# The inverse of each chunk's system multiplied into alpha and the values' side per unit, and a chain of two steps a chunk

## The chip, the core and the metric

The kernel runs on one core of a Trainium2 chip. The metric is device time in microseconds, from one execution of the whole program; the time before is the median of three runs, 2801.25 us (2798.41 to 2806.16). The core has five engines with queues of their own: TensorE (PE, matmuls), VectorE (DVE), ScalarE (ACT), GpSimd (POOL) and SyncE (SP, which here issues DMAs).

## What is computed

The reference is a trunk of two layers over 1024 positions of width 1024. The second layer's token mixer is a recurrence over positions, of 16 heads with a state of 64x64 each; the change touches only how that recurrence is computed.

```python
def wkv7_scan(r, w, k, v, a_, b_):
    # S_t = S_{t-1} diag(w_t) + (S_{t-1} a_t) b_t^T + v_t k_t^T ;  y_t = S_t r_t
    def step(S, inp):
        r_t, w_t, k_t, v_t, a_t, b_t = inp
        sa = jnp.einsum('bhij,bhj->bhi', S, a_t)
        S = S * w_t[:, :, None, :] + sa[..., None] * b_t[:, :, None, :] + v_t[..., None] * k_t[:, :, None, :]
        y = jnp.einsum('bhij,bhj->bhi', S, r_t)
        return S, y
    ...

def rwkv7_mixer(h, mu, w_in, w0, w1, w2, a0, a1, a2, g1, g2, k_k, k_a, r_k, ln_g, ln_b, w_out):
    ...
    y = wkv7_scan(rh, decay.reshape(B, T, H, N), kh, vh, -kk, kk * ah)
    ...
    return (y * g) @ w_out

    for i in range(DEPTH):
        ...
        if i % N_MIXERS == 0:
            mix = sgu_mixer(h, ...)
        else:
            mix = rwkv7_mixer(h, ...)
        x = x + gate1[:, None, :] * mix
        h = modulate(rms_norm(x), shift2, scale2)
        ff = jnp.square(jax.nn.relu(h @ mlp_w1[i])) @ mlp_w2[i]
        x = x + gate2[:, None, :] * ff
    return rms_norm(x) * final_g
```

## The kernel before

Around the recurrence the program is almost entirely matmuls with streamed weights: adaLN, the first layer and its MLP up to about 1215 us, then the recurrence with other work beside it up to about 2320 us, then the second layer's remaining output projection and MLP. All float32 products of the large matmuls are made from split high and low parts (`wh`, `wl`), three matmuls for one product.

The recurrence (`wkv`) is cut into 16 units: four quarters q of 256 positions (`NQ`, `N`) by four groups m of four heads. A unit has two pairs of heads (z), and each pair four chunks of 64 positions (`CS`). Within a chunk the recurrence is solved as a triangular system: `la` holds the masked products of alpha with the keys' side, `t` and `pf` its inverse, `uv` the solved vectors beside the values, `rr` the masked products for the output, `tm` the transposed key side, `st` or `S` the state.

Per unit there are generators: `unit_a` (decays, alpha and rho into `ar`, the products `pg` in banks g and m, masks into `la` and `rr`), `unit_e` (transposes and centred values), `unit_s` (the inverse of 16x16 blocks on DVE, by way of DRAM), `unit_b` (the inverse's larger blocks, in four half-steps of small matmuls and copies, ending with `pf`), `unit_c` (the chunk chain), `unit_d` (normalisation of the output, with a Ln and an Exp on ACT) and `unit_l` (loads). Each yields the place, in units, at which its next piece is due.

`interleave` merges them with a background generator `bg`: first the projections of the later quarters (`big`, `hidden`, `outs`), with weights read back from DRAM, then the output projection of the first half (`outp`) and most of its MLP (`half0`). A background piece of cost c moves the clock on by c / `RATES`[unit]. So a unit lasts 28.0 of the background's cost numbers (about microseconds of matmul) for the first ten, 41.5 afterwards, and a unit has 13 slots (`SLOT`). PE's instructions are pinned to this order (`Pinned`); the other engines' order is decided by the framework's scheduler, each engine works its own queue in order, and PE's queue waits whole when one operand is late.

The chain before has three steps a chunk, one slot each. In the first, PE adds `la` times `uv` (the values' side) and `ar` times the state into a bank of tag c, and ACT copies it to `xs`. In the second, PE multiplies `xs` by `pf` into tag c, and DVE (one pair) and ACT (the other) copy it to `uv`; the products of rho with the state for the output `y` stand beside it. In the third, PE multiplies `tm` with `uv`, adds `rr` times `uv` to `y`, and DVE makes the new state (`scalar_tensor_tensor` into `S`) from it and `sg`, the decayed state from POOL. Tag c has one buffer.

`outp` of quarter 0 starts when the four units of that quarter are through: `begin_x0` loads the residual into `hm` (tensor `xd`), `gated` reads the units' outputs back (`ev<-yd`), and ACT and DVE split them into `s`.

Of the kernel before, what the change touches and what calls it, by code (L numbers as in the profile page):

```python
# [108 lines left out]
class Trunk:  # L109
# [1074 lines left out]
    SLOT = 1 / 13  # L1184
    RATES = [28.0] * 10 + [41.5]

    def wkv(self, bg):
# [9 lines left out]
        self.ars = [u.tile([P, 8, 3, CS], F32, name=f"ar{i}") for i, u in enumerate(self.ups)]  # L1197
        nc.gpsimd.memset(self.ars[0], 0.0)
# [64 lines left out]
    def unit_0(self):  # L1263
# [11 lines left out]
        yield .5  # L1275
        nc.vector.memset(self.ars[1], 0.0)
# [5 lines left out]
    def unit_a(self, d):  # L1282
# [11 lines left out]
        g = self.own(d, "g", [8, CS + 1], 3)  # L1294
        G.memset(g[:, :, 0:1], 1.0)
        d["ar"] = ar = self.ars[d["n"] % 2]
# [3 lines left out]
        la = self.own(d, "la", [2, 8, CS])  # L1300
# [39 lines left out]
        G.tensor_tensor(ar[:, :, 2], c8(rp), g[:, :, 1:], ALU.mult)  # L1340
# [9 lines left out]
        for z in Z2:  # L1350
            t0 = (6 + z) * self.SLOT
            yield t0
            pg = [self.ps(t) for t in "gm"]
            for c in range(4):
                o = (c ^ z) * P
                cc = z * 4 + c
                for h, s in enumerate(HS):
                    PE.matmul(pg[h][:, o:o + P], bk[s, cc * 2:cc * 2 + 2].rearrange("p a t -> p (a t)"),
                              ar[s, cc, h::2 - h], start=True, stop=True)
# [7 lines left out]
        yield .59  # L1367
# [4 lines left out]
    def unit_e(self, d, z):  # L1372
# [5 lines left out]
        t0 = (8 + 2 * z) * self.SLOT  # L1378
# [8 lines left out]
        yield t0 + self.SLOT  # L1387
# [9 lines left out]
        yield t0 + self.SLOT + .02  # L1397
# [6 lines left out]
    def unit_s(self, d):  # L1404
# [4 lines left out]
        yield 0.61  # L1409
# [5 lines left out]
        yield 0.68  # L1415
        for i in range(1, NB):
# [6 lines left out]
            yield 0.68 + .017 * i  # L1423
        V.tensor_copy(tb[:, 1], tb[:, 0].rearrange("p s k -> p k s"))
        yield 0.96
# [3 lines left out]
        yield 1.0  # L1429
        d["t"] = self.ups[0].tile([P, 8, CS], F32, name="t")  # L1430
        for w, t in enumerate((d["t"], self.own(d, "pf", [8, CS]))):
# [12 lines left out]
    def unit_b(self, d):  # L1444
# [3 lines left out]
        at = lambda i: 1 + i * self.SLOT  # L1448
# [50 lines left out]

    def unit_c(self, d):  # L1500
# [4 lines left out]
        step = lambda i: 1 + (7 + i) * self.SLOT  # L1505
        yield step(0)
        ar, rr, tm, uv, la, pf, g = (d[x] for x in ("ar", "rr", "tm", "uv", "la", "pf", "g"))
# [4 lines left out]
        for c in range(4):  # L1512
# [3 lines left out]
            j = c // 2  # L1516
# [10 lines left out]
            sg = [self.ups[1].tile([P, CS], F32, name="sg", bufs=4) for _ in Z]  # L1527
            gc = [g[:, z * 4 + c, CS:CS + 1] for z in Z]
            for z in Z:
                G.tensor_scalar(sg[z], st[z], gc[z], None, ALU.mult)  # L1530
            yield step(3 * c + 1)
            pu = ht(self.ps("c"))
            for h in range(2):
                for z in Z:
                    PE.matmul(pu[ss[z], h], pf[ss[z], h * 4 + z * 2 + j], xs[ss[z], h], start=True, stop=True)
            for z in Z:
                for h, o in enumerate(HS):
                    PE.matmul(py[o, cc(z)], st[z][o], ar[o, z * 4 + c, 2], start=z == 0, stop=False)
# [11 lines left out]
            for z in Z:  # L1550
                V.scalar_tensor_tensor(ns[z], pq[:, z * CS:z * CS + CS], gc[z], sg[z], ALU.mult, ALU.add)
# [242 lines left out]
```

## Time and profile before

| what | value |
|---|---|
| median of three runs | 2801.25 us |
| the profiled execution | 2805.26 us, of which span 2803.5 us |
| PE busy | 2613.3 us (93%) |
| PEld, DVE, ACT, POOL busy | 2152.6, 1638.3, 1146.9, 544.7 us |
| chain that ended last | PE 67%, DVE 12%, DMA 11%, ACT 4% |
| mean granted clock | 0.969 |

The page gives busy time, a 40-slice map and the chain of waits. The recurrence lies in slices 18 to 33, from about 1215 to 2320 us. The views used are the busy time by stretch, the list of who PE waited for, and the engines' instructions in order of time. A float32 matmul appears there as two pieces, each a load and a matmul; where several pieces of the same kind follow, a row has their count. PE's rows are modelled at their ends, so a cost is read from start to start.

### The profile page before, as it was taken

How to read it: one execution, taken by the hardware profiler on the slowest of the kernel's cores; microseconds unless marked ns; L12 is line 12 of the kernel's file. 1: busy time of each engine (PE TensorE's matmuls, PEld its weight loads, DVE VectorE, ACT ScalarE, POOL GpSimd, SP SyncE). 2: the span in 40 equal slices, each digit the busy share in tenths (PEclk: the TensorE clock that was granted, in tenths of full speed). 3: DMA queues.
4: the chain of work that ended last, by engine and by line, in shares of the span. 5: the costliest groups of instructions: out<-in, count | busy, mean ns of one | idle time of the engine just before them, and what ended most of it. 6: DMA issues, size and time to landing. Idle time of an engine off the chain costs nothing.

```text
span 2803.5 us, 49454 instructions
## 1 busy us (share of the span) xinstructions
PE 2613.3 (93%) x19020; PEld 2152.6 (77%) x19020; DVE 1638.3 (58%) x3066; ACT 1146.9 (41%) x2074; POOL 544.7 (19%) x574
## 2 busy tenths in 40 slices
PE   6999999999999999787898997879999999999998
PEld 4788888877888788787787886777777778788887
DVE  7856775444333458866666663566667545744445
ACT  4523442333311344553454543464444334533333
POOL 1000000433300013431322231123334220100001
PEclk9999999999999999998999999899999999999999
DMA  7644545888711354788888889753333324333332
GB/s 279 211 142 128 167 155 163 274 278 255 237 49 49 91 165 138 241 291 261 260 284 265 270 289 274 211 149 110 104 104 100 91 86 151 103 109 94 95 94 83
DMA packets 369708, 483.67 MB, mean 173 GB/s; under 512 B 144320, under 2 KB 153536, under 8 KB 368704
## 3 DMA queue, kind: packets, MB, share of 16 engines
q1 hardware_dynamic: 354496, 454.18, 52.3%
q10 hardware_dynamic: 14976, 26.34, 2.5%
q8 instruction: 149, 2.44, 0.4%
q14 instruction: 87, 0.71, 0.1%
HBM read 390.07 MB, written 90.32 MB: 171 GB/s over the span
## 4 chain that ended last, share of the span: by engine, by line
PE 67%; DVE 12%; DMA 11%; ACT 4%; issue 4%; SPq 1%; POOL 1%; ACTq 0%; DVEq 0%; POOLq 0%
PE acc L448 24%; PE acc L646 15%; PE acc L103 15%; PE c L103 2%; PE acc L503 2%; DMA split<-ada_acc 2%; PE t L103 2%; DMA split<-araw 2%; DVE pr L1420 2%; DVE hm L874 2%; PE acc L894 1%; DVE wl L407 1%; DMA araw<-in_ada_w 1%; DVE xi L440 1%; DMA lb<-ltd 1%
## 5 line engine op out<-in xcount | busy, mean ns | idle before, releaser
L448 PE MATMUL acc<-h,wh 128*128 128x512 f32 x2112 | 667.4, 397 | 0.0
L401 ACT CAST wh<-raw 128x512 fp32r<-128x512 f32 x517 | 318.6, 619 | 732.6 <-PE acc L448 299.0
L646 PE MATMUL acc<-s,wh 128*128 128x512 f32 (+1 forms) x1664 | 510.4, 389 | 12.1 <-DVE s L439 9.1
L407 DVE TENSOR_TENSOR wl<-raw,wh 128x512 fp32r<-128x512 f32 x475 | 363.1, 767 | 264.4 <-ACT wh L401 259.3
L448 PEld LDWEIGHTS acc<-h,wh 128*128 128x128 f32 x2112 | 394.9, 188 | 94.5 <-issue 1.2
L448 PE MATMUL acc<-h,wl 128*128 128x512 f32 x1056 | 418.0, 396 | 0.0
L646 PEld LDWEIGHTS acc<-s,wh 128*128 128x128 f32 x1664 | 308.9, 189 | 86.5 <-DVE s L439 14.8
L646 PE MATMUL acc<-s,wl 128*128 128x512 f32 (+1 forms) x832 | 323.1, 389 | 0.5 <-DVE wl L407 0.5
L452 DVE SCALAR_TENSOR_TENSOR x<-acc,mod,x 128x512 f32<-128x512 f32 (+1 forms) x224 | 163.1, 730 | 231.0 <-PE acc L646 206.4
L448 PEld LDWEIGHTS acc<-h,wl 128*128 128x128 f32 x1056 | 198.4, 188 | 48.0 <-issue 0.5
L103 PE MATMUL acc<-s,wh 128*128 128x512 f32 (+1 forms) x616 | 188.0, 390 | 35.0 <-ACT s L437 18.3
L407 POOL TENSOR_TENSOR wl<-raw,wh 128x512 fp32r<-128x512 f32 (+1 forms) x107 | 145.6, 1363 | 318.2 <-ACT wh L401 156.2
L103 PE MATMUL acc<-xi,wh 128*128 128x256 f32 (+1 forms) x896 | 179.5, 300 | 10.0 <-ACT hm L954 5.2
L646 PEld LDWEIGHTS acc<-s,wl 128*128 128x128 f32 x832 | 157.5, 189 | 35.3 <-DVE wl L407 1.2
L358 POOL TENSOR_TENSOR araw<-araw,ada_acc 128x512 fp32r<-128x512 f32 (+1 forms) x78 | 101.2, 1300 | 389.4 <-ACT ada_acc L355 354.1
L103 PEld LDWEIGHTS acc<-s,wh 128*128 128x128 f32 x616 | 111.0, 196 | 62.8 <-ACT s L437 18.8
L103 PEld LDWEIGHTS acc<-xi,wh 128*128 128x128 f32 (+1 forms) x896 | 144.3, 198 | 17.7 <-ACT hm L954 5.4
L103 PE MATMUL acc<-h,wh 128*128 128x512 f32 (+1 forms) x512 | 150.7, 381 | 3.2 <-ACT ev L1057 3.2
L103 PE MATMUL acc<-xi,wl 128*128 128x256 f32 (+1 forms) x448 | 129.8, 290 | 1.6 <-issue 0.8
L355 ACT CAST ada_acc<-araw 128x512 fp32r<-128x512 f32 (+1 forms) x80 | 49.4, 618 | 168.4 <-DMA split<-ada_acc 124.3
L103 PE MATMUL acc<-s,wl 128*128 128x512 f32 (+1 forms) x308 | 114.9, 373 | 0.0
L157 DVE SCALAR_TENSOR_TENSOR ada_acc<-araw,cond,ada_acc 128x512 f32<-128x512 f32 x140 | 104.4, 746 | 13.0 <-DMA araw<-in_ada_w 11.1
(269 smaller groups left out, 4415.8 us busy)
## 6 DMA issues: line engine op xcount, KB each, us to landing
raw<-in_mlp_w SPq DMA_DIRECT2D x432, 256.0 KB, 2.7
araw<-in_ada_w SPq DMA_DIRECT2D x192, 256.0 KB, 3.5
raw<-split SPq DMA_DIRECT2D x142, 256.0 KB, 4.9
wh<-split SPq DMA_DIRECT2D x141, 256.0 KB, 4.6
wl<-split SPq DMA_DIRECT2D x141, 256.0 KB, 4.7
split<-ada_acc SPq DMA_DIRECT2D x76, 256.0 KB, 3.8
split<-araw SPq DMA_DIRECT2D x76, 256.0 KB, 4.1
araw<-in_w_in SPq DMA_DIRECT2D x48, 256.0 KB, 3.8
```

The lines of the kernel that those rows point to most:

```text
L103: self.tc.keep_in_program_order(self.pe.matmul(*a, **k))
L157: nc.vector.scalar_tensor_tensor(acc, raw, self.cond[:, k:k + 1], acc, ALU.mult, ALU.add)
L355: nc.scalar.copy(hi[:rows, :m].bitcast(F32R), raw[:rows, :m])
L358: nc.gpsimd.tensor_tensor(to[lo, :m].bitcast(F32R), raw[lo, :m], hi[lo, :m], ALU.subtract)
L401: (nc.vector.tensor_copy if self.nhi % 3 == 0 and self.shared else nc.scalar.copy)(wh[:rows], raw[:rows])
L407: eng.tensor_tensor(wl[:rows], raw[:rows], rd(wh[:rows]), ALU.subtract)
L448: nc.tensor.matmul(ps, w[s](k), x[m][:, k], start=n == 0, stop=n == 3 * KC - 1)
L452: self.nc.vector.scalar_tensor_tensor(x[:, e], ps, gate[:, e:e + 1], x[:, e], ALU.mult, ALU.add)
L503: self.nc.tensor.matmul(ps, h[s][:, k, ts], self.wv[k][m], start=k + i == 0, stop=k + i == KC + 1)
L646: nc.tensor.matmul(ps, w[:, k], s[hf, k][:, i, ts], start=n == 0, stop=n == 3 * FB - 1)
L874: nc.vector.scalar_tensor_tensor(t[:, z], self.hx[:, e + z], self.mu[:, i, e + z:e + z + 1], self.h[:, e + z, 1:], ALU.mult, ALU.add)
L1420: V.tensor_tensor(pr[:, :i, :i], lb[:, 0:i, i].unsqueeze(1).to_broadcast([64, i, i]), tb[:, 0, 0:i, 0:i].rearrange("p s k -> p k s"), ALU. ...
```

## The change

Two products that the chain made for each chunk are made for a whole unit, ahead of its chain, by a new generator `unit_x`. It first transposes alpha (bank m, tile `at`) and multiplies `la` by the values' side (bank g, tile `x0`); once `pf` is finished it multiplies `at` by `pf` (banks t and r), which four ACT copies place into `au`, a zeroed tile, and `pf` by `x0` (bank c), which ACT copies to `u0`. The chain's first step is then `au` times the state, with DVE adding `u0` while writing `uv`; `xs` is gone, and a chunk has two steps. The products of rho move into the first step. The other engines' small changes: one full-width multiplication for alpha in place of two half-height ones, and a POOL copy of the chunk-end decays (`gc`). `la`, `pf` and `g` have one buffer, alpha one and rho two.

The grid is ninths of a unit: a chain step is due every 1/9 (it was 1/13), the half-steps of `unit_b` every 1/18 (1/13), the two parts of `pg` 1/9 apart (1/13). The rates go to 27.4 and 42.0. The due places of the other pieces move a little with it: `unit_s` starts 0.04 to 0.06 of a unit later, `unit_d` 0.01 to 0.05 earlier.

```diff
-    SLOT = 1 / 13
-    RATES = [28.0] * 10 + [41.5]
+    SLOT = 1 / 9
+    RATES = [27.4] * 10 + [42.0]
...
-        self.ars = [u.tile([P, 8, 3, CS], F32, name=f"ar{i}") for i, u in enumerate(self.ups)]
-        nc.gpsimd.memset(self.ars[0], 0.0)
+
+        self.ar = ua.tile([P, 3, 8, CS], F32, name="ar")
+
+
+        self.au = ub.tile([P, 4, 2, 2, CS], F32, name="au")
+        nc.gpsimd.memset(self.au, 0.0)
...
-                  self.unit_c(d), self.unit_d(d)]
+                  self.unit_x(d), self.unit_c(d), self.unit_d(d)]
...
-        for i, s in enumerate(HS):
-            V.scalar_tensor_tensor(ar[s, :, i], c8(kk)[s], -(2.0 ** -8), g[s, :, 0:CS], ALU.mult, ALU.mult)
-            yield 0.35 + .02 * i
+        V.scalar_tensor_tensor(al, c8(kk), -(2.0 ** -8), g[:, :, 0:CS], ALU.mult, ALU.mult)
+        yield 0.36
+        G.tensor_copy(gc, g[:, :, CS])
...
-            t0 = (6 + z) * self.SLOT
+            t0 = (4 + z) * self.SLOT
...
-        t0 = (8 + 2 * z) * self.SLOT
+        t0 = (6 + z) * self.SLOT
...
-        at = lambda i: 1 + i * self.SLOT
+        at = lambda i: 1 + (i + 2) / 2 * self.SLOT
...
+    def unit_x(self, d):
+
+
+        nc = self.nc
+        S, PE = nc.scalar, self.pe
+        Z = range(2)
+        HS, LO, HI = self.HS, self.LO, self.HI
+        ss = lambda c, z: HS[c + z & 1]
+        tile = lambda name, *sh: self.ups[0].tile([P, *sh], F32, name=name)
+        yield 8 * self.SLOT
+        la, uv, pf = d["la"], d["uv"], None
+
+        pa = self.ps("m").rearrange("p (c t) -> p c t", c=4)
+        for c in range(4):
+            for z in Z:
+                PE.matmul(pa[ss(c, z), c], self.ar[:, 0, z * 4 + c], self.ident, start=True, stop=True)
+        px = self.ps("g").rearrange("p (c h t) -> p c h t", c=4, h=2)
+        for c in range(4):
+            for h in range(2):
+                for z in Z:
+                    sv = ss(c, 1 - z)
+                    PE.matmul(px[ss(c, z), c, h], la[sv, h, z * 4 + (c ^ z)], uv[sv, z * 4 + c, h], start=True, stop=True)
+        yield 8 * self.SLOT + .015
+        at, x0 = tile("at", 4, P), tile("x0", 4, 2, CS)
+        S.copy(at, pa)
+        S.copy(x0, px)
+        yield 1 + 4.5 * self.SLOT
+        pf = d["pf"]
+
+        pp = [self.ps(t) for t in "tr"]
+        for c in range(4):
+            for i in range(2):
+                for z in Z:
+                    h = (c + z + i) & 1
+                    PE.matmul(pp[i][HS[h], c * CS:c * CS + CS], at[ss(c, z), c, h * CS:h * CS + CS],
+                              pf[ss(c, z), h * 4 + z * 2 + c // 2], start=True, stop=True)
+        pu = self.ps("c").rearrange("p (c h t) -> p c h t", c=4, h=2)
+        for c in range(4):
+            for h in range(2):
+                for z in Z:
+                    PE.matmul(pu[ss(c, z), c, h], pf[ss(c, z), h * 4 + z * 2 + c // 2], x0[ss(c, z), c, h],
+                              start=True, stop=True)
+        yield 1 + 4.5 * self.SLOT + .015
+        for i in range(2):
+            pc = pp[i][:, :4 * CS].rearrange("p (c t) -> p c t", c=4)
+            for h, o in enumerate(HS):
+                S.copy(self.au[o, :, h ^ i, h], pc[o])
+        d["u0"] = tile("u0", 4, 2, CS)
+        S.copy(d["u0"], pu)
...
-        step = lambda i: 1 + (7 + i) * self.SLOT
+        step = lambda i: 1 + (5 + i) * self.SLOT
...
-            px = ht(self.ps("c"))
-            for h in range(2):
-                for z in Z:
-                    sv = ss[1 - z]
-                    PE.matmul(px[ss[z], h], la[sv, h, at(z)], uv[sv, z * 4 + c, h], start=h == 0, stop=False)
-            for h in range(2):
-                for z in Z:
-                    PE.matmul(px[ss[z], h], ar[:, z * 4 + c, h], st[z], start=False, stop=h == 1)
-            xs = self.ups[1].tile([P, 2, CS], F32, name="xs", bufs=2)
-            S.copy(xs, px)
...
-            yield step(3 * c + 1)
             pu = ht(self.ps("c"))
             for h in range(2):
                 for z in Z:
-                    PE.matmul(pu[ss[z], h], pf[ss[z], h * 4 + z * 2 + j], xs[ss[z], h], start=True, stop=True)
+                    PE.matmul(pu[ss[z], h], self.au[:, c, c + z & 1, h], st[z], start=True, stop=True)
...
             for z in Z:
-                (S.copy if z else V.tensor_copy)(uv[ss[z], z * 4 + c], pu[ss[z]])
-            yield step(3 * c + 2)
+                V.tensor_tensor(uv[ss[z], z * 4 + c], pu[ss[z]], u0[ss[z], c], ALU.add)
+            yield step(2 * c + 1)
...
-        yield 2 + 6 * self.SLOT
+        yield 2 + 4 * self.SLOT
```

On PE, around the end of a late unit's inverse and the start of its chain (`r` is the bank of `unit_d`'s matmul with `ysq`, `t` with `w` the last half-step of `unit_b`, rows of `acc` are background). Before:

```order
L103 MATMUL r<-ysq,bones 128x512
L103 MATMUL t<-pf_22787,w_23124 32x32 x16
L103 MATMUL g<-ar_10432,bk 128x128
...
L103 MATMUL c<-uv_22049,la_22050 64x64 x4
L103 MATMUL c<-st_8569,ar_10431 64x64
...
L103 MATMUL c<-xs,pf_22787 64x64 x4
L103 MATMUL y<-ar_10431,st_8569 64x64 x2
```

After:

```order
L103 MATMUL r<-ysq,bones 128x512
L103 MATMUL t<-pf_23240,w_23531 32x32 x16
L103 MATMUL g<-ar,bk 128x128
...
L103 MATMUL t<-pf_23240,at 64x64 x2
L103 MATMUL r<-pf_23240,at 64x64 x2
...
L103 MATMUL c<-x_23147,pf_23240 64x64 x16
...
L103 MATMUL c<-st_8569,au 64x64
L103 MATMUL c<-st_8570,au 64x64
...
L103 MATMUL y<-ar,st_8569 64x64 x2
```

The first product that reads the finished `pf` stands one chain step and two stretches of background behind the last half-step before; now it stands behind `pg` and nine background matmuls, and the chain's first step follows twelve background matmuls later.

On ACT, at the same place of the same unit. `ysq` with TABLE_LOAD ahead is Ln, then Exp, of `unit_d`; `pf` from `t` 32x8x32 is the end of the inverse. Before:

```order
L1488 COPY w_23124<-t 32x256
L401 CAST wh<-raw 128x512
L1572 ACT_TABLE_LOAD
L1572 ACTIVATE ysq<-r,eps_gn 128x512
L1575 ACT_TABLE_LOAD
L1575 ACTIVATE ysq<-ysq 128x512
L1498 COPY pf_22787<-t 32x8x32
L401 CAST wh<-raw 128x512
L1526 COPY xs<-c 128x128
L401 CAST wh<-raw 128x512
L1540 COPY uv_22049<-c 64x128
```

After:

```order
L1493 COPY w_23531<-t 32x256
L401 CAST wh<-raw 128x512
L1615 ACT_TABLE_LOAD
L1615 ACTIVATE ysq<-r,eps_gn 128x512
L1618 ACT_TABLE_LOAD
L1618 ACTIVATE ysq<-ysq 128x512
L1503 COPY pf_23240<-t 32x8x32
L401 CAST wh<-raw 128x512
L1551 COPY au<-t 64x4x64 x2
L1551 COPY au<-r 64x4x64 x2
L1553 COPY u_23651<-c 128x512
```

The copy of `pf` stands behind Ln and Exp in both; now the four copies of `au` and the copy of `u0` stand behind it, ahead of the chain's first step.

On SP, where the output projection of quarter 0 starts: `tpd<-tb` stores the blocks of the inverse that DVE has made, `t<-tpd` and `pf<-tpd` read them back, `hm<-xd` loads the residual, `ev<-yd` the gated outputs, the rest are weights. Before:

```order
L1428 DMA tpd_257<-tb 64x16x16 x2
L326 DMA wl<-split_1_232 128x512
L1133 DMA hm<-xd 128x1024
L1433 DMA t<-tpd_257 64x8x64 x2
L1433 DMA pf_17741<-tpd_257 64x8x64 x2
L1133 DMA hm<-xd 128x1024 x3
L995 DMA ev<-yd_8607 128x512 x3
```

After:

```order
L1133 DMA hm<-xd 128x1024
L1433 DMA tpd_257<-tb 64x16x16 x2
L326 DMA wh<-split_0_225 128x512
L326 DMA wl<-split_1_226 128x512
L1438 DMA t<-tpd_257 64x8x64 x2
L1438 DMA pf_17980<-tpd_257 64x8x64 x2
L326 DMA raw<-split_1_228 128x512
L326 DMA wh<-split_0_229 128x512
L326 DMA wl<-split_1_230 128x512
L326 DMA wh<-split_0_231 128x512
L326 DMA wl<-split_1_232 128x512
L995 DMA ev<-yd_8607 128x512 x3
```

The store and the loads of the inverse, which stood between the last weights and the gated outputs together with all four loads of the residual, now stand five weight loads ahead of them, and one load of the residual there, the others further ahead.

## Rows read from the trace of the kernel before

**Rows 1.** Busy time by stretch: stretch, us, busy us of PE, PEld, DVE, ACT, POOL; PEclk, DMA share, GB/s
```profile
1215.00:1735.00 520.00, 458.83 (x6020) 414.57 (x6020) 316.34 (x784) 252.71 (x500) 134.52 (x162) 0.94 0.88 278
1885.00:2320.00 435.00, 422.31 (x4279) 324.85 (x4279) 266.30 (x591) 182.21 (x352) 152.49 (x163) 0.99 0.37 102
```
**Rows 2.** Who PE waited for, 1215 to 1885 us: us in total, times, longest
```profile
PE acc L103 <- ACT s L437: 20.2, 3, 17.2
...
PE c L103 <- DVE S L1551: 9.5, 8, 2.7
PE c L103 <- ACT uv L1540: 6.4, 4, 3.0
...
PE g L103 <- DVE rr L1365: 3.8, 3, 2.4
```
**Rows 3.** The same view, 1885 to 2320 us
```profile
PE t L103 <- ACT pf L1476: 1.8, 2, 0.9
...
PE c L103 <- ACT uv L1540: 1.5, 1, 1.5
```
**Rows 4.** PE in order of time, one chunk: start us, us, instruction, count
```profile
2271.83 0.63 PE L103 MATMUL acc<-s,wh 128*128 128x512 f32 x2
2272.30 0.39 PE L103 MATMUL acc<-s,wl 128*128 128x512 f32 x1
2272.62 0.45 PE L103 MATMUL c<-uv,la 64*64 64x64 f32 x8
2273.00 0.45 PE L103 MATMUL c<-st,ar 128*64 128x64 f32 x8
2273.38 0.73 PE L103 MATMUL acc<-s,wh 128*128 128x512 f32 x2
2273.95 0.40 PE L103 MATMUL acc<-s,wl 128*128 128x512 f32 x1
...
2276.06 0.40 PE L103 MATMUL acc<-s,wl 128*128 128x512 f32 x1
2276.38 0.45 PE L103 MATMUL c<-xs,pf 64*64 64x64 f32 x8
2276.66 0.40 PE L103 MATMUL y<-ar,st 64*64 64x64 f32 x8
2276.99 0.73 PE L103 MATMUL acc<-s,wh 128*128 128x512 f32 x2
```
**Rows 5.** PE in order of time, six full-width pieces of 128 columns
```profile
1718.22 0.83 PE L103 MATMUL t<-bcent,v 128*128 128x128 f32 x6
1718.81 0.36 PE L103 MATMUL acc<-hr,raw 128*128 128x256 f32 x1
```
**Rows 6.** Busy time by stretch as in rows 1, three stretches after a wait
```profile
1396.90:1403.80 6.90, 6.72 (x104) 6.26 (x106) 2.03 (x4) 0.53 (x2) 4.45 (x6) 0.51 0.96 326
1499.30:1502.80 3.50, 3.50 (x29) 3.38 (x26) 3.47 (x11) 2.10 (x5) 0.00 (x0) 0.51 0.37 140
1564.20:1571.00 6.80, 6.49 (x51) 5.94 (x51) 6.33 (x18) 2.13 (x5) 0.80 (x2) 0.50 0.63 205
```
**Rows 7.** PE, then SP, in order of time, where the first output projection starts
```profile
1751.08 1.31 PE L103 MATMUL acc<-s,wh 128*128 128x256 f32 x2 [17.18 <-ACT s L437]
...
1733.99 1.30 SPq L1428 DMA_DIRECT2D tpd<-tb  x2
...
1743.68 1.52 SPq L995 DMA_DIRECT2D ev<-yd  x3
```
**Rows 8.** ACT in order of time behind one unit's matmul with `ysq`
```profile
1470.49 1.28 ACT L1572 ACT_TABLE_LOAD   x1
1471.79 0.69 ACT L1572 ACTIVATE ysq<-r,eps_gn 128x512 f32<-128x512 f32 x1
...
1474.44 0.36 ACT L1498 COPY pf<-t 32x256 f32<-32x256 f32 x1
```
**Rows 9.** ACT by line and shape: count, busy us, mean ns, idle before it
```profile
L1399 ACT COPY uv<-t 64x256 f32<-64x256 f32 x30 | 11.0, 367 | 34.3 <-PE t L103 33.6 <-ACT ev L985 0.4
```

More of the change, by code (lines that the diff above doesn't have):

```diff
@@ L1293, in unit_a @@
         ew, ea = wa[:, 0], wa[:, 1]
-        g = self.own(d, "g", [8, CS + 1], 3)
+        g = self.own(d, "g", [8, CS + 1], 1)
         G.memset(g[:, :, 0:1], 1.0)
-        d["ar"] = ar = self.ars[d["n"] % 2]
+        pair = slice(0, 2 + d["n"] % 2, 1 + d["n"] % 2)
+        al, rho = self.ar[:, 0], self.ar[:, 1 + d["n"] % 2]
+        d["rho"] = rho
+        gc = self.own(d, "gc", [8])
         rr = self.own(d, "rr", [8, 2, CS])
@@ L1299, in unit_a @@
         self.own(d, "uv", [8, 2, CS])
-        la = self.own(d, "la", [2, 8, CS])
+        la = self.own(d, "la", [2, 8, CS], 1)
         d["bk"] = bk = self.ut.tile([P, 16, CS], F32, name="bk")
@@ L1339, in unit_a @@
         yield .33
-        G.tensor_tensor(ar[:, :, 2], c8(rp), g[:, :, 1:], ALU.mult)
+        G.tensor_tensor(rho, c8(rp), g[:, :, 1:], ALU.mult)
         for z, zs, _, p in Z:
@@ L1358, in unit_a @@
                     PE.matmul(pg[h][:, o:o + P], bk[s, cc * 2:cc * 2 + 2].rearrange("p a t -> p (a t)"),
-                              ar[s, cc, h::2 - h], start=True, stop=True)
+                              self.ar[s, pair, cc], start=True, stop=True)
             yield t0 + .02
@@ L1408, in unit_s @@
         NB = self.NB
-        yield 0.61
+        yield 0.65
         ld = d["ld"]
@@ L1414, in unit_s @@
         pr = self.ups[0].tile([64, NB, NB], F32, name="pr")
-        yield 0.68
+        yield 0.74
         for i in range(1, NB):
@@ L1428, in unit_s @@
             nc.sync.dma_start(self.blocks(td, w), tb[:, w])
-        yield 1.0
+        yield 1.05
         d["t"] = self.ups[0].tile([P, 8, CS], F32, name="t")
-        for w, t in enumerate((d["t"], self.own(d, "pf", [8, CS]))):
+        for w, t in enumerate((d["t"], self.own(d, "pf", [8, CS], 1))):
             for h, s in enumerate(self.HS):
@@ L1504, in unit_c @@
         Z = range(2)
-        step = lambda i: 1 + (7 + i) * self.SLOT
+        step = lambda i: 1 + (5 + i) * self.SLOT
         yield step(0)
-        ar, rr, tm, uv, la, pf, g = (d[x] for x in ("ar", "rr", "tm", "uv", "la", "pf", "g"))
+        rho, rr, tm, uv, u0, gc = (d[x] for x in ("rho", "rr", "tm", "uv", "u0", "gc"))
         at = lambda z: z * 4 + (c ^ z)
@@ L1534, in unit_c @@
                 for z in Z:
-                    PE.matmul(pu[ss[z], h], pf[ss[z], h * 4 + z * 2 + j], xs[ss[z], h], start=True, stop=True)
+                    PE.matmul(pu[ss[z], h], self.au[:, c, c + z & 1, h], st[z], start=True, stop=True)
             for z in Z:
                 for h, o in enumerate(HS):
-                    PE.matmul(py[o, cc(z)], st[z][o], ar[o, z * 4 + c, 2], start=z == 0, stop=False)
+                    PE.matmul(py[o, cc(z)], st[z][o], rho[o, z * 4 + c], start=z == 0, stop=False)
+            sg = [self.ups[1].tile([P, CS], F32, name="sg", bufs=4) for _ in Z]
+            gz = [gc[:, z * 4 + c:z * 4 + c + 1] for z in Z]
             for z in Z:
-                (S.copy if z else V.tensor_copy)(uv[ss[z], z * 4 + c], pu[ss[z]])
-            yield step(3 * c + 2)
+                G.tensor_scalar(sg[z], st[z], gz[z], None, ALU.mult)
+            for z in Z:
+                V.tensor_tensor(uv[ss[z], z * 4 + c], pu[ss[z]], u0[ss[z], c], ALU.add)
+            yield step(2 * c + 1)
             pq = self.ps("c")
@@ L1550, in unit_c @@
             for z in Z:
-                V.scalar_tensor_tensor(ns[z], pq[:, z * CS:z * CS + CS], gc[z], sg[z], ALU.mult, ALU.add)
+                V.scalar_tensor_tensor(ns[z], pq[:, z * CS:z * CS + CS], gz[z], sg[z], ALU.mult, ALU.add)
             st = ns
-            yield step(3 * c + 3) if c < 3 else step(11) + .01
+            yield step(2 * c + 2) if c < 3 else step(7) + .01
         y = d["y"] = self.late("y")
```

31 lines of the change are left out of this document (12 added, 19 removed).

## The prediction

> **What bounds the kernel now.** I read the busy time by stretch first. Over the whole span TensorE (PE) is 93% busy; beside the recurrence it is idle 61 us of 520 up to 1735 us and 13 of 435 from 1885 on [rows 1]. So late units cost what their matmuls cost, and early units that and waits. DMA is at 0.88 in the early stretch, yet few PE waits end on a transfer; the waits list names copies and sums on ACT and DVE. There I look for the waits that the change can move [rows 2, 3]. The chain's own are 9.5 us for the state S (8 waits), 6.4 and 1.5 us for `uv` (5). Next the clock: three stretches right behind such waits, 17.2 us together, ran at 0.50 to 0.51, the level of 1.2 GHz, after PE had stood idle in such a wait, the longest 2.7 and 3.0 us [rows 2, 6]; their matmuls would have needed half the time. Last, one wait has nothing to do with the chain's length: 17.2 us, where the first output projection starts [rows 2, 7].
>
> **The chain's matmuls, taken away: -51 us.** In the late chunk, background matmuls of 512 columns start 0.235 us apart (two take 2271.83 to 2272.30). From the last one before the first step to the next one behind it are 1.08 us, so the step costs 0.85, and 0.10 more because the two matmuls behind it take 0.57 rather than 0.47 [rows 4]. The second step costs 0.93 - 0.235 + 0.10 = 0.80 [rows 4]; the third has as many pieces of the same shape as the second and stays. After the change a first step with `au` (8 pieces, the shape of `st,ar`) and the products of rho (8 pieces, the other shape) replaces two steps. It is built like the old first step, 8 pieces of each shape, so I give it 0.95. That leaves 0.80 a chunk, times 64 chunks.
>
> **The new unit_x on PE: +65 us (58 to 78).** A piece of 64 columns costs 0.029 us when they run two abreast: the 8 of `y` take 0.33 us, less 0.10 to leave [rows 4]. Alone, a piece of 128 columns takes 0.59 / 6 = 0.098 us [rows 5]. First part: the 16 pieces of the transposed alpha, 128 columns in two halves of the output; two abreast 0.8 us, one by one 1.6. Then 32 pieces of `la` with `uv`, 0.93. A change of shape costs 0.10: the 8 pieces of `la` take 0.38 up to `ar`, those of `xs` 0.28 up to `y` [rows 4]. It stands right behind a chain step, so it pays no entrance. Sum 1.85. Second part: 64 pieces at 0.029 make 1.86, entrance and exit 0.33 (what the second step costs beyond its 16 pieces); 2.2, or 1.7 if four pieces of the first half run abreast, in two banks and four quarters of the array, of which no row shows a case. Together 4.05 us a unit (3.6 to 4.9), times 16. I take two abreast, since every group of 64-column pieces in rows 4 does it. PE's net is +14 us (+7 to +27).
>
> A rule speaks against this. The rows show 8 pieces of `xs` by `pf`, from both halves of the partitions into one bank, 0.035 us apart, entrance counted, where one after another they would take 0.05 [rows 4, 5]. The Trainium skill, TensorEngine Tiling (Array Packing), section Restrictions and Gotchas, says that different row tiles cannot access the same PSUM bank simultaneously. By that rule the unit's 96 pieces of 64 columns would cost 4.8 us instead of 2.8, and PE's net would be +46 us instead of +14; the trace speaks against it for the old chain, and the new products are the same shapes.
>
> **The chain's waits: -15 us, and the clock behind them: -8.** A step was due every 28.0 / 13 = 2.15 of the background's cost numbers, and is now due every 27.4 / 9 = 3.04. The same answer of DVE or ACT therefore has two fifths more background to hide behind, and the chunk has two answers instead of three. `uv` now comes from DVE alone, which adds `u0` there. The listed waits of 17.4 us are 1.3 us each on average and 3.0 at most; I keep 2 us (bounds: all stay, none stays). Of the 17.2 us at half clock, half comes back, 8.6; I take 8. The two parts of `pg` move apart in the same way, from 2.15 to 3.04, and the second waits for DVE to empty bank g (3.8 us [rows 2]): -3 (0 to -4).
>
> **The start of the output projection: -10 us (0 to -14).** Before, SP stood until 1733.99 for DVE's blocks (`tpd<-tb`), then issued the inverse's loads and the residual's, and reached `ev<-yd` at 1743.68; PE started at 1751.08 after 17.18 us [rows 7]. With 27.4 for 28.0 the background comes to this place later in the units, and SP has the inverse's store and loads, and three of the residual's four, behind it. Without them the first gated outputs could be asked for about when PE runs dry. What remains is a transfer and a split: 1743.68 to 1751.08 is 7.4 us before, with the residual's loads just ahead. So 7 of 17 stay. What is late next is the third output, whose buffer waits for the last store of a projection.
>
> **New waits: +14 us, and +3 for the clock behind them.** Three places have less cover.
> - The half-steps of the inverse come every 1.52 instead of 2.15. Each needs a copy on ACT or DVE; late units already wait for `pf` there (1.8 us in two waits [rows 3]). I take +5 (0 to +12).
> - The product with finished `pf`. Its copy stands on ACT behind Ln and Exp with their table loads: 4.3 us from the first load to its end [rows 8]. The first load waits for the matmul with `ysq` in ten of 15 units, by the order. PE meanwhile has the 32 pieces of the half-step (0.6 us), `pg` (about 1.2) and 8 to 15 background matmuls, 3.3 to 4.9 us in all. Before, a chain step more stood between, and this copy made no one wait. Now up to 1 us a unit is open: +6 (0 to +15).
> - The four copies into `au`. The nearest row is a 64x256 copy at 0.367 us [rows 9], so 1.5 us, with at times casts between them; PE covers them with the products for `u0` (0.9) and at least 1.4 us of background: +3 (0 to +16).
> The clock can fall behind these as it fell behind the old ones: +3 (0 to +14). DVE and POOL gain and lose small pieces off the path; they cost nothing while DVE is at 61% in both stretches [rows 1].
>
> **Sum.** -51 + 65 - 15 - 8 - 3 - 10 + 14 + 3 = -5 us, against the profiled execution of 2805.26 us, so 2800 there. That execution lay 4.0 us above the median of the three runs, 2801.25; on that scale the forecast is **2796 us**.
>
> **Rivals.**
> - *The cover holds.* The new copies are hidden, the projection starts as soon as its data are there, four pieces run abreast. PE +7, chain waits -17, clock -9, bank g -4, projection -14, new waits +3: -34, so 2767 us. For it: the units whose tables load early need only 3 us. Against it: ACT's queue around the inverse's end is dense.
> - *ACT becomes the bound at the turn of each unit.* If Ln and Exp start late, the copy of `pf` and those of `au` are late in every unit: +15 and +16 in place of +6 and +3, the clock +14 in place of +3. That is 33 us more, 2829 us. It decides from the point where the end of the `pf` copy, 4.3 us behind `ysq`, lies beyond PE's 3.3 to 4.9 us. For it: cover is 3.3 us in several early units. Against it: five of 15 units load the table ahead.
> - *The chain's waits are DVE's queue, not the chain.* Then they stay although a step is dropped, with their clock: 15 + 8 = 23 us more, 2819 us; the change would not do what it says. Against it: the longest wait, 3.0 us, is near what the wider step adds.
> - *The 64-column pieces of unit_x do not pair.* 96 times 0.021 us, 16 units: 32 us more, 2828 us. This is the result of the page's rule above; rows 4 bear against it.
>
> **How the numbers follow.** About 0.3%, 8.4 us, is what a measurement of this kernel can tell from no change. The forecast has 0.55; its own range, 2780 to 2812, holds 0.19 of faster, 0.33 of the same and 0.03 of slower. The cover holds: 0.21, faster. ACT as the bound 0.12, the waits stay 0.08, no pairing 0.04, all slower. So faster 0.40, same 0.33, slower 0.27. The range reaches from the first rival to just beyond the waits that stay, 2768 to 2822; what it leaves out is part of these two ends, about 2 in 10.
>
> **What would show it.** In the profile after: pieces of `c` from `la` and `xs` gone from the chain, one chain step near 0.95 and one near 0.80 us; unit_x near 4 us a unit, its 64-column pieces 0.029 apart; waits for S and `uv` under 3 us in sum; a wait under 10 us at the first `acc<-s` behind 1700 us; waits at the products with `at` and at the chain's first step of about 9 us in sum, released by ACT. The forecast is wrong if those last waits reach 25 us, if idle PE in the early stretch does not fall, or if unit_x costs 6 us.

## The result and the profile after

The changed kernel takes 2824.11 us (median of 6 runs, 2814.04 to 2824.98) where the kernel before, in as many runs beside it, takes 2804.86: ratio 1.0066 (95% interval 1.0049 to 1.0083). On another chip it was 1.0065 (1.0040 to 1.0091). Slower by 19 us; the forecast was 5 us faster.

The profiled execution took 2820.74 us. Its page: span, busy time by engine, the granted clock in tenths.

```profile
span 2819.0 us, 51133 instructions
...
PE 2630.3 (93%) x19788; PEld 2172.3 (77%) x19788; DVE 1650.0 (59%) x3113; ACT 1160.9 (41%) x2057; POOL 544.2 (19%) x590
...
PEclk9999999999999999999989998899999999999999
```

The two stretches of [rows 1], in the same columns:

```profile
1215.00:1735.00 520.00, 460.66 (x6342) 416.76 (x6342) 313.52 (x778) 259.38 (x493) 127.85 (x166) 0.92 0.86 273
1885.00:2320.00 435.00, 416.57 (x4453) 326.00 (x4454) 268.63 (x608) 183.62 (x336) 153.09 (x167) 0.98 0.37 99
```

In this trace PE's idle time beside the recurrence is 59 us early (61 before) and 18 late (13 before), and the clock is lower in both. In the two later traces of the changed kernel the early stretch has 69 us idle (63 in the second of before), at the clock of before, 0.94. Whom PE waited for, 1215 to 1900 us (total us, times, longest), answers [rows 2]:

```profile
PE acc L103 <- ACT s L437: 16.8, 2, 10.8
...
PE c L103 <- ACT u L1553: 10.5, 4, 7.6
...
PE t L103 <- ACT pf L1503: 3.2, 4, 1.2
...
PE c L103 <- DVE uv L1583: 2.3, 5, 0.8
PE t L103 <- ACT w L1467: 2.2, 2, 2.0
PE t L103 <- ACT pf L1481: 2.0, 4, 1.0
...
PE c L103 <- DVE S L1594: 0.7, 2, 0.4
```

The same, 1900 to 2340 us, answers [rows 3]:

```profile
PE t L103 <- ACT pf L1481: 5.3, 2, 3.3
PE t L103 <- ACT w L1467: 3.9, 1, 3.9
PE t L103 <- ACT pf L1503: 2.8, 4, 1.5
```

The chain's waits went as planned: 17.4 us for S and `uv` became 3.0. The wait for bank g's `rr` is gone. In their place, where one unit's inverse ends and its chain begins (the turn of the unit), stand 30 us: 13.4 in the half-steps (`pf` L1481, `w`), 6.0 at the product with finished `pf` (L1503), and 10.5 at the chain's first matmul, for `u`.

That last one was not in the forecast, and 7.6 of its 10.5 us stand at a single turn of the sixteen. PE in order of time there:

```profile
1536.66 0.27 PE L103 MATMUL t<-pf,at 64*64 64x64 f32 x2
1536.67 0.27 PE L103 MATMUL r<-pf,at 64*64 64x64 f32 x2
...
1537.17 1.10 PE L103 MATMUL c<-x,pf 64*64 64x64 f32 x32
1538.20 1.61 PE L103 MATMUL acc<-xi,raw 128*96 128x256 f32 x12
1547.44 0.69 PE L103 MATMUL c<-st,au 128*64 128x64 f32 x8 [7.63 <-ACT u L1553]
```

ACT in the same stretch (in brackets how long it stood idle ahead of the instruction, and for whom):

```profile
1535.47 0.63 ACT L1618 ACTIVATE ysq<-ysq 128x512 f32<-128x512 f32 x1
1536.13 0.37 ACT L1503 COPY pf<-t 32x256 f32<-32x256 f32 x1
1541.07 0.62 ACT L437 CAST xi<-hm 128x512 fp32r<-128x512 f32 x1 [4.57 <-DVE hm L874]
1541.71 0.36 ACT L1551 COPY au<-t 64x256 f32<-64x256 f32 x1
...
1544.70 0.41 ACT L437 CAST hr<-hm 128x256 fp32r<-128x256 f32 x1 [1.05 <-DVE hm L955]
1545.13 0.37 ACT L1551 COPY au<-r 64x256 f32<-64x256 f32 x1
1546.16 0.62 ACT L437 CAST xi<-hm 128x512 fp32r<-128x512 f32 x1 [0.66 <-DVE hm L874]
1546.80 0.58 ACT L1553 COPY u<-c 128x512 f32<-128x512 f32 x1
```

The product is finished at 1538.2, and ACT is idle, yet its copies stand behind casts of the background, which wait for DVE: 4.57, 1.05 and 0.66 us. DVE in the same stretch:

```profile
1536.14 2.08 DVE L1622 SCALAR_TENSOR_TENSOR ysq<-y,bvec,ysq 128x256 f32<-128x256 f32 x2 [1.62 <-ACT ysq L1618]
1538.15 1.26 DVE L1625 SCALAR_TENSOR_TENSOR ysq<-ysq,bvec,v 128x256 f32<-128x256 f32 x1
...
1539.99 1.78 DVE L874 SCALAR_TENSOR_TENSOR hm<-hm,mu 128x256 f32<-128x256 f32 x4
```

It is at the previous unit's group norm, which waited for ACT's own Exp, and comes to `hm` behind it. The chain's first matmul needs bank c, which `pu` holds until the copy `u` has read it.

### The profile page after: what moved, and what is told of

Read it like the earlier page. It is cut to its first block, busy times and chain, and to the rows that moved or that the text cites. A ratio compares the mean times of both kernels' runs of the same rounds, so it can differ in the third digit from the quotient of the medians.

```text
span 2819.0 us, 51133 instructions
## 1 busy us (share of the span) xinstructions
PE 2630.3 (93%) x19788; PEld 2172.3 (77%) x19788; DVE 1650.0 (59%) x3113; ACT 1160.9 (41%) x2057; POOL 544.2 (19%) x590
## 4 chain that ended last, share of the span: by engine, by line
PE 66%; DMA 12%; DVE 11%; ACT 5%; issue 4%; SPq 1%; POOL 1%; ACTq 0%; DVEq 0%; POOLq 0%
PE acc L448 24%; PE acc L646 16%; PE acc L103 15%; DMA split<-araw 2%; DMA split<-ada_acc 2%; PE t L103 2%; PE acc L503 2%; DVE pr L1425 2%; PE c L103 1%; PE g L103 1%; DVE wl L407 1%; DVE hm L874 1%; DMA araw<-in_ada_w 1%; DMA wl<-split 1%; PE acc L894 1%
## 5 line engine op out<-in xcount | busy, mean ns | idle before, releaser
L103 PEld LDWEIGHTS acc<-xi,wh 128*128 128x128 f32 (+1 forms) x896 | 144.8, 199 | 20.2 <-ACT ev L989 7.8
L103 PE MATMUL acc<-xi,raw 128*128 128x256 f32 (+1 forms) x672 | 101.5, 298 | 12.3 <-ACT hm L954 6.0
```

The costliest lines, as they stand in the source:

```text
L103: self.tc.keep_in_program_order(self.pe.matmul(*a, **k))
```

## Where the time went

Both programs have the same 11,020 background matmuls, so the trace can be cut at the same ones. The table takes the time between the starts of the 4350th and the 9600th (1108 and 2481 us before) apart: idle stretches of PE above 0.15 us; half of PE's time at half clock, idle stretches left out; the time from a background matmul's start to the next one's where small ones stand between, less these two; the rest. The third kind holds the background matmul ahead of each interruption, which cancels in the table, with 226 interruptions before and 225 after. Before is the mean of two traces, after of three.

| us | before | after | difference | forecast |
|---|---|---|---|---|
| small matmuls (chain, product, half-steps) | 341.2 | 350.9 | +9.7 | +14 |
| PE idle | 135.2 | 138.9 | +3.7 | -14 |
| lost at half clock | 56.4 | 52.6 | -3.9 | -5 |
| background itself | 836.8 | 839.7 | +2.9 | 0 |
| ahead of the 4350th | 1.0 | 6.2 | +5.1 | 0 |

(The last row counts from the first trace of before.) The sum is +17.5. So the work came out nearly as forecast, and PE's idle and half-clock time together did not fall: 191.6 before, 191.5 after.

## Experiments

**Second traces.** The start of the recurrence, at 1108.0 us in the first trace of before:

> The kernel before once more, for a second trace. In the first pair of traces the changed kernel is already 6.8 us later when the recurrence starts, at 1108 us, in work that the change does not touch. Theory turn-of-unit (the added time lies in the recurrence, in new waits on ScalarE where one unit ends and the next begins): the start of the recurrence here lies within 2 us of the first trace, and the lag of 6.8 us is in the changed kernel only or in chance. Rival accident: the start of the recurrence differs from the first trace by 3 to 7 us, so the lag says nothing of the change.

> The changed kernel once more, for a second trace. Accident: its start of the recurrence moves toward that of the kernel before, by 3 to 7 us. Rival placement (the change moves buffers, and so slows work ahead of the recurrence): the same 6 to 7 us late again, in the same two places (by 163 us and by 620 us). Turn-of-unit: TensorE's waits for ScalarE's copies u, pf and w inside the recurrence are again 25 to 35 us together.

2.1 us later in the second trace of before; 3.5 us later in that of after (6.8 in the first), and the waits for `u`, `pf` and `w` are again 30 us. Neither theory on the lag was clean.

**The rates alone, in the kernel before.**

```diff
-    RATES = [28.0] * 10 + [41.5]
+    RATES = [27.4] * 10 + [42.0]
```

> The kernel before with the two pacing rates of the changed kernel alone. Forecast of the prediction: the wait at the first output projection (17.2 us in one piece) falls to between 7 and 17, and the kernel gains up to 10 us: about 2797. Rival, the rates only move the wait: the sum of the waits for the split of the output projection stays at 20 us and the time within 3 us of 2805. Against the change: the units are paced a little slower in rate, so the chain steps get closer to one another than 28.0 gave; if that costs more, 2808 or more.

0.9926 (0.9903 to 0.9950), 2781.94 us against 2803.09: twice the gain that the prediction gave the rates, and not where it put it. Waits, 1215 to 1900 us:

```profile
PE acc L103 <- ACT s L437: 16.5, 2, 13.1
...
PE c L103 <- DVE S L1551: 7.3, 5, 2.4
...
PE c L103 <- ACT uv L1540: 2.9, 3, 2.1
```

The projection's start (20.2 and 17.7 in two traces of before) gave 1 to 4 us; the chain's waits went from 17 to 19 down to 10.2. PE idle fell by 15 us to 120.3 and the half-clock loss by 7 to 49.8.

**A bank of its own for `pu`.**

```diff
-        pp = [self.ps(t) for t in "tr"]
+        pp = [self.ps(t) for t in "tg"]
...
-        pu = self.ps("c").rearrange("p (c h t) -> p c h t", c=4, h=2)
+        pu = self.ps("r").rearrange("p (c h t) -> p c h t", c=4, h=2)
```

> The changed kernel with the product of the finished inverse and the values' side in a bank of its own (it had the chain's bank c, which the chain's first matmul then waits for until ScalarE has copied it out). Theory turn-of-unit: the wait of c for u, 10.5 us in 4 pieces, goes; what is left is a wait for the four copies of au, 1 to 4 us; with the half-speed stretch behind it 6 to 10 us less: 2814 to 2818. Rival, cover only moved: the chain then waits as long for the au copies (7 us or more) or for the add of u0 on VectorE, and the time stays within 3 us of 2824.

1.0093 (1.0074 to 1.0112), no faster. The wait for `u` is gone, and PE stops earlier, at the product with `at`, for bank g, which DVE has not emptied. Waits, 1215 to 1900 us:

```profile
PE g L103 <- DVE rr L1370: 13.5, 8, 2.9
...
PE c L103 <- ACT au L1551: 3.5, 2, 2.6
```

**The old rates, bank y, a later group norm, and the grid alone.** These ran on one chip. First:

```diff
-    RATES = [27.4] * 10 + [42.0]
+    RATES = [28.0] * 10 + [41.5]
```

> The changed kernel with the two pacing rates of the kernel before (28.0 and 41.5). In the kernel before, the new rates alone took 21 us off (2782). Theory, the rates are worth as much in either program: 2845 here. Rival, their worth lay in the old chain's waits (c<-S, uv and s, which the changed chain hardly has): 2820 to 2830, no change that can be told.

1.0078 (1.0061 to 1.0094): the rates make no difference that can be told in the changed kernel. Second:

```diff
-        pu = self.ps("c").rearrange("p (c h t) -> p c h t", c=4, h=2)
+        pu = self.ps("y").rearrange("p (c h t) -> p c h t", c=4, h=2)
...
-                    PE.matmul(py[o, cc(z)], st[z][o], rho[o, z * 4 + c], start=z == 0, stop=False)
...
             yield step(2 * c + 1)
+            if c == 0:
+                py = self.ps("y")
...
+                        PE.matmul(py[o, cc(z)], st[z][o], rho[o, z * 4 + c], start=z == 0, stop=False)
```

> The changed kernel with the product of the inverse and the values' side in bank y, and the y matmuls of a unit's first chunk moved behind its first step's VectorE add, so that neither the chain's first matmul nor bank g (which made 20 us of waits for VectorE's rr when the product's pieces stood in it) waits for more than before. Theory turn-of-unit: the wait for u (10.5 us) goes, 2 to 4 us for the au copies stay, and with the clock behind it 6 to 10 us less: 2814 to 2818. Rival, whatever is late at the turn is late for another reason (ScalarE's order of work behind VectorE): the waits come back at au, y or acc, and the time stays within 3 us of 2824.

1.0055 (1.0041 to 1.0070), which overlaps the changed kernel's interval. The rival was nearer: without the wait for `u` PE stands 5.5 us in the same place for the copies of `au`, 5.2 of it at the turn shown above, and idle and half-clock time come to 196 us.

```profile
PE c L103 <- ACT au L1551: 5.5, 2, 5.2
```

Third:

```diff
-        yield 2 + 4 * self.SLOT
+        yield 2 + 4 * self.SLOT + .09
...
-        yield 2.46
+        yield 2.55
```

> The changed kernel with the group norm of the unit before (its matmul, logarithm, exponential with their two table loads on ScalarE, and what follows) 0.09 of a unit later, behind the copies at the turn of the unit. Theory, the finished inverse waits behind these two table loads: the waits t<-pf at the product (6 us in 8) and part of u go, 5 to 9 us less: 2815 to 2819. Rival, ScalarE is held by casts that wait for VectorE, not by the table loads: waits as before, 2821 to 2827; the later store costs nothing in either.

1.0069 (1.0053 to 1.0085): nothing. `pf` fell to 7.8 us and `u` went, and 7.0 us for `au` came at bank r, where the norm's matmul now waits, 6.4 of it at that same turn:

```profile
PE r L103 <- ACT au L1551: 7.0, 2, 6.4
```

(The norm's last add here reads its values after a later unit's have been loaded over them; the work is the same.) Fourth, in the kernel before with the new rates (`GRID` is 1/9):

```diff
-            t0 = (6 + z) * self.SLOT
+            t0 = (4 + z) * self.GRID
...
-        at = lambda i: 1 + i * self.SLOT
+        at = lambda i: 1 + (i + 2) / 2 * self.GRID
```

> The kernel before with the new rates and, of the grid, all but the chain: masked products, transposes, solve and the four half-steps of the inverse at the places that the changed kernel gives them (ninths, half-steps at half a ninth), the chain as before with three steps a chunk. No product outside the chain. Theory, the half-steps placed closer cost by themselves: waits t<-pf and t<-w of 10 to 15 us appear, and 2782 becomes 2792 to 2800. Rival, they wait only when the product's copies stand on ScalarE as well: 2778 to 2786. Third, it costs nearly the whole 40 us between this kernel with the new rates and the changed one: 2810 or more.

1.0035 (1.0019 to 1.0052), 2808.98 us, but the runs spread from 2795 to 2820. The waits for `pf` were 6.1 us, `w` none, fewer than the first theory asked. Something had not been counted: two grids that don't fit one another interrupt the background 333 times instead of 226 (225 in the changed kernel). That costs little by itself: 8.7 us more among the small matmuls, but they hold 107 background matmuls more, and the background is 3.2 us less, so 5 to 6 us. Most of the loss stands in idle and half-clock time, 195 us against 170 and 161 with the new rates alone. In all it is 25 to 31 us (1.0035 less 0.9947 or 0.9926), without `unit_x` and with the old chain, where the whole change costs 33 to 39 against the same rates. By the ratio that is 2815 us on the scale of the first pair, the third range: nearly the whole loss. How much of it belongs to the two grids together, which the changed kernel does not have, is not shown.

**The solve and the half-steps earlier.**

```diff
-        yield 0.74
+        yield 0.69
...
-        at = lambda i: 1 + (i + 2) / 2 * self.SLOT
+        at = lambda i: 1 + (i + 1) / 2 * self.SLOT
...
-        yield 1 + 4.5 * self.SLOT
+        yield 1 + 4.25 * self.SLOT
```

> The changed kernel with the solve, the four half-steps of the inverse and the group norm's logarithm half a ninth of a unit earlier, and the product a quarter of a ninth earlier: the same work in the same places of VectorE, ScalarE and TensorE, with half a ninth more between the last half-step and the chain. Theory turn-of-unit: the waits for pf, w and u (30 us in the first traces of the changed kernel) fall by 10 to 20 us, and the time to 2802 to 2812. Rival, the solve moved earlier is now awaited itself (t<-tpd and w grow by as much): 2818 to 2826.

1.0001 (0.9986 to 1.0016), 2798.40 us: it takes the whole loss back. Waits, 1215 to 1900 us, then 1900 to 2340:

```profile
PE t L103 <- DMA t<-tpd: 13.3, 8, 5.8
PE acc L103 <- ACT s L437: 12.3, 3, 6.9
...
PE c L103 <- ACT u L1553: 5.3, 2, 4.3
```

```profile
PE t L103 <- ACT pf L1481: 3.7, 4, 1.7
PE t L103 <- ACT w L1467: 2.8, 3, 1.3
```

The 30 us at the turn are 12, part of it back as waits for the solve itself (`t<-tpd`, 13.3; 7.7 in the changed kernel). With bank y on top:

> The last kernel and the product's second half in bank y with the y matmuls of the first chunk later, together. The bank alone brought 2814.5. Theory turn-of-unit: the two gains add, 2796 to 2806. Rival, each takes away the same lateness: no better than the better of the two, 2808 to 2815. The kernel before with the new rates (2782) stays ahead in all of these, by the 10 us of TensorE work that the change adds.

1.0005 (0.9992 to 1.0019). `u` is gone again, and nothing is gained again.

**Rates further, and the product twice.**

```diff
-    RATES = [28.0] * 10 + [41.5]
+    RATES = [26.8] * 10 + [42.5]
```

> The kernel before with rates further along the same way (26.8 and 42.5 where the new ones are 27.4 and 42.0). If the 21 us came from a trend (fewer waits of the chain while the projections run beside it, more of their work left for the units behind), 2765 to 2780; if 27.4 just happens to put the units' work at good places between the background's evictions, 2785 to 2805.

0.9966 (0.9953 to 0.9979): better than 28.0 and not better than 27.4, whose second interval it just overlaps. No trend. And in the changed kernel, in all four loops of `unit_x`:

```diff
-        for c in range(4):
+        for c in (*range(4), *range(4)):
```

> The changed kernel with each matmul of the product outside the chain issued twice into the same place: the product's TensorE work doubled, nothing else. In the trace it costs 3.75 us a unit (1.95 for the first part, 1.80 for the second). Theory, TensorE is the bound wherever it does not wait, so this work is paid in full: 50 to 65 us more, 2872 to 2885. Rival, part of it fills waits that are there anyway (for the output projection's split, for evictions): 25 to 45 us, 2847 to 2865. If the waits at the turn grow with it, 70 us or more.

1.0235 (1.0211 to 1.0259), 47 us above the changed kernel's 1.0066, between the two ranges that were expected. In the trace the small matmuls grew by 49 us, not by the 60 of the expectation, and PE's idle time hardly fell (131 us; 134 to 144 in three traces of the changed kernel). Idle time here is no slack into which more matmuls would fit; it stays, and work is added to it.

**Four more on one chip**, for what was still open.

> The kernel before with the new rates once more, on the chip that also runs the next three. If the 21 us are the rates', 0.990 to 0.995 of the kernel before again; if they were that chip's or that placement's chance, above 0.996.

0.9947 (0.9928 to 0.9966): the gain is the rates'.

> The kernel before with the first rate changed alone (27.4, and 41.5 as before). Two thirds of the gain of the two rates stood behind the ten units that run beside the projections (at the turn to the output projection and after). The prediction gave the rates 10 us, all at the wait of the output projection's split (17 us), which fell only to 13. Theory, the first rate makes it (the units come a little earlier, and the chain and the output projection's own evictions meet less): 2778 to 2788. Rival, the second rate, in the units beside the output projection: 2792 to 2802.

0.9968 (0.9950 to 0.9985): the first rate gives about half of it. That is less than the theory asked and inside the rival's range; no run has the second rate alone.

> The changed kernel with the solve and half-steps half a ninth earlier, and the rates of the kernel before. The rates made no difference to the changed kernel (2820 with the old ones), whose lateness at the turn hid everything else. If they count once the turn is not late: 2808 to 2820, some 10 to 20 us more than with the new ones (2798). If they were only good for the old chain: 2793 to 2803.

1.0070 (1.0049 to 1.0091): the rates do count once the turn is not late, and the earlier solve without them is worth nothing, although the waits at the turn are as short as with them (`pf` 4.9, `w` 3.7, `u` 3.0). PE waits 16 us for weights still in transfer (`raw`, `wl`, `wh`; 11 with the new rates), and 69 us are lost at half clock (60 with them).

> The changed kernel a third time, on the chip of the last three, for the difference between them on one chip and for a third trace of the work ahead of the recurrence. If the lag of 3 to 7 us by 1108 us belongs to the program: again a granted clock of 0.95 between 570 and 720 us where the kernel before has 0.98. If it is chance: 0.97 or more. The time against the earlier-solve variant: 15 to 25 us more than it, in waits for pf, w and u.

1.0065 (1.0040 to 1.0091), with 31 us at the turn and the lag at 8.2 us. The lag goes with a stretch ahead of the recurrence. Stretch 570 to 720 us, columns as in [rows 1]: before, after, and after with bank y.

```profile
570.00:720.00 150.00, 140.18 (x582) 111.14 (x581) 65.80 (x75) 52.14 (x91) 56.83 (x44) 0.98 0.85 269
```

```profile
570.00:720.00 150.00, 138.47 (x565) 109.51 (x564) 65.00 (x74) 51.98 (x91) 54.38 (x42) 0.95 0.82 259
```

```profile
570.00:720.00 150.00, 142.29 (x595) 112.81 (x595) 67.05 (x77) 52.45 (x92) 56.78 (x45) 0.98 0.84 270
```

All three traces of the changed kernel and six of its eight variants have 0.94 or 0.95 there, the two with bank y 0.98; of seven traces of the kernel before and its variants six have 0.97 or 0.98, and the one with the first rate 0.95. The instructions up to there are the same in all. It belongs to the program rather than to the run, but not to anything that the change says; why, stays open.

**All kernels in one table**: ratio to before, small matmuls, and PE's idle and half-clock time together, in the stretch of the table above.

| kernel | ratio | small | idle + half clock |
|---|---|---|---|
| before (two traces) | 1 | 341, 342 | 195, 188 |
| before, new rates (two) | 0.9926, 0.9947 | 340, 340 | 170, 161 |
| before, first rate / rates further | 0.9968 / 0.9966 | 340 / 339 | 181 / 185 |
| before, new rates and grid | 1.0035 | 348 | 195 |
| after (three) | 1.0066, 1.0065 | 351, 351, 351 | 192, 190, 193 |
| after, old rates | 1.0078 | 351 | 185 |
| after, bank r / bank y | 1.0093 / 1.0055 | 354 / 350 | 196 / 196 |
| after, norm later | 1.0069 | 348 | 188 |
| after, solve earlier / and bank y | 1.0001 / 1.0005 | 348 / 349 | 179 / 178 |
| after, solve earlier, old rates | 1.0070 | 349 | 197 |
| after, product twice | 1.0235 | 400 | 193 |

## Why the prediction was wrong, point by point

- **Chain matmuls -51: right.** In a late chunk, PE in order of time:

```profile
2252.36 0.40 PE L103 MATMUL acc<-h,wl 128*128 128x512 f32 x1
2252.68 0.45 PE L103 MATMUL c<-S,au 128*64 128x64 f32 x8
2253.07 0.45 PE L103 MATMUL y<-ar,S 64*64 64x64 f32 x8
2253.44 0.74 PE L103 MATMUL acc<-h,wh 128*128 128x512 f32 x2
2254.02 0.39 PE L103 MATMUL acc<-h,wl 128*128 128x512 f32 x1
```

  2253.44 - 2252.36 - 0.235 = 0.85, and 0.10 behind it: 0.95, as forecast.
- **unit_x +65: 59.** A first part right behind a chain step costs 1.95 us (1.85 forecast): 2.66 for the interruption less 0.71 for the step. The second costs 1.75 (2.2 forecast): in the rows of the turn, 32 pieces of `at` by `pf` take 0.51 us in two banks and four quarters, the case that no row of before had shown, and the 32 of `x` by `pf` 1.03. At 0.032 us each, two starting 0.007 us apart and the next two 0.052 us later, they pair, and the fourth rival fell. With it fell the rule of the Trainium skill, TensorEngine Tiling (Array Packing), section Restrictions and Gotchas, that different row tiles cannot access the same PSUM bank simultaneously, as the prediction applied it: these pieces go from both halves of the partitions into separate halves of one bank. PE's net is +9.7 (+14 forecast); 16 times 3.70 less 51 is 8.
- **Chain waits -15, bank -3, clock -8 and +3: right.** S and `uv` went from a mean of 18.2 us to 4.8 (three traces), `rr` in banks g and m from 5.6 to none. Half-clock time fell by 3.9.
- **Start of the output projection -10: -3.** The premise failed. Before PE's first matmul there, on PE and then SP:

```profile
1764.13 1.31 PE L103 MATMUL acc<-s,wh 128*128 128x256 f32 x2 [10.80 <-ACT s L437]
```

```profile
1752.48 1.28 SPq L1438 DMA_DIRECT2D t<-tpd  x2
...
1758.08 2.07 SPq L995 DMA_DIRECT2D ev<-yd  x3
```

  PE ran dry at 1753.3, and SP was still at the inverse's loads; they had not moved away from the place. The transfer and split took 6.05 us, near the 7.4 of before. A second wait of 6.0 us followed.
- **New waits +14: 27.** The product waited 6.0 us, as forecast. The half-steps, at 1.52 of the background's cost numbers instead of 2.15, waited 13.4 us. Before it was 2.8, the line for `pf` in [rows 3] and these two, from 1215 to 1885 and 1885 to 2320 us:

```profile
PE t L103 <- ACT pf L1476: 0.3, 1, 0.3
```

```profile
PE t L103 <- ACT w L1462: 0.7, 1, 0.7
```

  So 10.6 were added, where I took 5 and bounded it at 12. And `pu` in bank c was costed at nothing, because I looked for who reads `u0` (DVE) and not for who needs its bank. `au` itself, +3, cost nothing: the wait for `u` covers it. Of the signs that the prediction named against itself one showed: idle PE in the early stretch hardly fell, 61 to 59 us, and in the later traces it rose to 69.
- **The rival nearest in mechanism**, ACT as the bound at the turn, said 2829. Its waits came (16.5 of 30 at the product and the chain's first step), its clock did not, and its mechanism was only half right: at the turn shown ACT is not busy but stands behind DVE. Two more rivals lay as near in number by luck: 2828, if the pieces did not pair, and they pair; 2819, if the chain's waits stayed, and they fell.
- **The steps that failed are two terms of the sum.** Forecast and traces lie 22 us apart (-5 and +17.5). The new waits make 13 of that: the wait for bank c, 10.5 us, was put at nothing, and the half-steps at 5 where they added 10.6. The start of the output projection makes 7, because the inverse's loads did not leave the place. The lag ahead of the recurrence and the background add 8, and the other terms give some 6 back. The listed waits do add up to the idle time: -13, -6, -3 and +27 make 5, and PE's idle time rose by 3.7.
- **What the experiments add: a listed wait has no price of its own.** Three edits took the 10.5 us wait for `u` away, and none gained it (1.0055, 1.0069 and 1.0093 against 1.0066). At the old rates the earlier solve brought the waits at the turn from 33 us to 12, and the time stayed (1.0078, 1.0070). PE's order is fixed, and when one late result no longer stopped it, the next one did, or the clock fell: with bank y PE idled 132 us instead of 139, and 64 us instead of 53 were lost at half clock. The sum of the two stayed between 185 and 197 us in all twelve traces of the kernel before and of the kernels clearly slower than it, and placement alone moves it: 26 us (191.6 to a mean of 165.7) by rates changed by 2 and 1%. That the same lateness of ACT and DVE is met again at the next instruction is shown for banks g and r and for `au`; for the rest it is argued.
- **What stays open**: why 27.4 is a good rate, and why the earlier solve needs it. Both probably belong to how the units' work falls among the background's, but no run takes one such meeting apart. Nor has any run `unit_x` and the short chain at the old places, so what they cost apart from the new grid is shown for their matmuls alone.

The version that beats both is the kernel before with the two rates alone, 0.9926 and 0.9947. Against it the change costs 33 to 39 us as it stands (1.0066 less either ratio), and 15 to 21 with the solve earlier; 10 of these are matmuls.

## What to carry to other kernels

Where PE's order is pinned and other engines lag it, a wait in the list names where the lag was met, not what it costs; here matmul time was paid nearly at its price, and of the waits that were taken away only those of the earlier solve with the new rates were gained. When a new result gets a buffer, ask first who needs that buffer next. And when a change carries new pacing numbers, try the numbers alone: here they gained 15 to 21 us by themselves, nothing that could be told within the change, and the rest of the change costs 22 at the old rates (1.0078).

## What the runs showed of the hardware

Four quarters of the array ran abreast in two banks at 0.016 us a piece of 64 columns, four starts 0.007 us apart and the next four 0.039 later, against 0.032 for two halves in one bank. Work added to PE beside a recurrence in which it is idle 10% of the time (139 of 1382 us) was paid almost whole: 47 us for 49 us of matmuls.
